# FFN output of a two-layer encoder trunk: x's sums added by on-chip transfers, and m2, v and h of two groups in shared banks

## Chip, cores and metric

The kernel runs on one core of one Trainium2 chip, as one program. The metric is the device time of one execution in microseconds (us), median of three runs. A profiled execution gives the trace: start and duration of every instruction on TensorE (PE; PEld is its weight load), VectorE (DVE), ScalarE (ACT), GpSimd (POOL), and the transfers issued from SyncE's queue (SP) and from POOL's.

## The reference

Two layers, each a token mixer with three branches and then a feed-forward network (FFN), on x of 512 rows by 1024 columns in float32. The part that the change touches is the second half of each layer:

```python
x = _layer_norm(DEEPNORM_ALPHA * x + mix, ln1_g[l], ln1_b[l])
u = jnp.einsum('bsd,df->bsf', x, w_ffn_in[l])
u_gate, u_up = jnp.split(u, 2, axis=-1)
ffn = jnp.einsum('bsf,fd->bsd', jax.nn.silu(u_gate) * u_up, w_ffn_out[l])
x = _layer_norm(DEEPNORM_ALPHA * x + ffn, ln2_g[l], ln2_b[l])
```

The hidden width is 2816, that is 22 tiles of 128. The last product, hidden (512 x 2816) by w_ffn_out (2816 x 1024), and the layer norm behind it are what is rearranged.

## The kernel before

**Numbers.** Each float32 operand is carried as a pair hi + lo, and each product of tiles is three matmuls, hi·hi, hi·lo and lo·hi (mm3, L120 to L122). A weight block is loaded into a staging buffer (tile st) and split: ScalarE casts it to hi (tile wh, L267, or L152 for blocks of w_ffn_in and w_in), then VectorE subtracts for lo (tile wl, L268 or L153). There are four staging buffers (NSTAGE) and three pairs wh and wl (AHEAD).

**Fewer products.** The hidden tiles are cut into three groups of consecutive tiles (GROUPS): 8, 8 and 6 tiles, called o, w and r here as in the code. In each group, the left operand and the weights are cut into 2 x 2 blocks, and seven products are formed in place of eight: m1, m2, y, x, v, g, h. Each is made twice (j = 0, 1, one for each tile of 128 rows of a half), into one PSUM bank of 128 x 512 (tile pf). With kh = 4 tiles of depth a product takes 2 x 12 matmuls, in r with kh = 3 it takes 2 x 9. The combinations of hidden tiles for the left side are made in s_hid (L300 to L303 and L112).

**Weights of a product.** Some products need sums of weight blocks. They are made by transfers that add onto a staging buffer: `load` (L172, SP's queue) brings a block, `more` (L176, POOL's queue, accumulating) adds another onto it. In a group's chain (class Chain, Fore for r) one staging buffer lives from m1 (Chain) or from `ahead_a` (Fore) to h: y, x and h each split it, and y and x then add the next block. `ahead_c` prepares the sum for g in a second buffer. m2 and v (and m1 of Fore) load a block each into whatever buffer is free, and release it when VectorE has split it.

**Sums.** z holds the rows of x: four tiles t of 128 rows, each in two halves hf of 512 columns. `plus` (L1316, or L1314 when a half of z is first touched and scaled by ALPHA) adds a bank or a tile onto a half of z on VectorE. m1 and y copy their banks to SBUF (tiles w and wy, L1341 and L1348, ScalarE). x computes u = x - m1 (L1354), adds it to z[2+j][0], then y + u (L1356), adds that to z[2+j][1] and z[j][1]. m2, v, g and h add their banks straight onto z. With the last product that touches a half, its statistics are taken (bn, L481). When both halves of a tile are there, it is normalised: `normalise` in layer 0 (L498 to L503, with one operation on POOL, L501), `finish` in layer 1 (L486 to L493, POOL L489), which also sends the rows out (L494).

**Order.** `items` is a list written out by hand: each entry names its weight blocks, the product, and groups of side work that are put between its two j or behind it. `run_items` fetches (loads and splits) blocks up to three ahead. A scheduler then places the instructions of each engine; SP's and POOL's queues run in their order as well. For w and r the order of products is: w.m1, u(19), w.y, u(20), w.x, u(21), w.m2, w.v, r.m1, r.y, w.g, r.m2, r.x, r.v, w.h, r.g, r.h. Here u(i) is a hidden tile of the first FFN product (u_ffn, 48 matmuls). In layer 0, s_norm(0) and s_norm(1), the transposes of the finished tiles 0 and 1 for the next layer (tile px, L512) and their split (to_T), stand between the two j of w.h and behind it; the next layer's first products need them.

```python
def take(self, i, j):
    b = self.block(self.a)
    self.more(self.a, i, j)
    return b
...
self.hi = wsp.tile([P, 2048], F32R, tag="wh", name="wh")[:, :n].rearrange("p (k c) -> p k c", k=nk)
...
nc.scalar.copy(self.hi, st)
nc.vector.tensor_sub(self.lo, st, f(self.hi))
```

Of the kernel before, what the change touches and what calls it, by code (L numbers as in the profile page):

```python
# [15 lines left out]
ALU = mybir.AluOpType  # L16

P = 128
# [36 lines left out]
def trunk(ctx, tc, x_in, xT_in, w_in, ret_norm_g, da_norm_g, lq1, lk1, lq2, lk2, w_a, w_b, w_c, b_merge, w_out,  # L55
          ln1_g, ln1_b, w_ffn_in, w_ffn_out, ln2_g, ln2_b, rel, rope_ret, rope_da, decay, out):
    nc = tc.nc
# [23 lines left out]
    def bank(name="ps"):  # L81
        return psp.tile([P, 512], F32, tag="ps", name=name)
# [36 lines left out]
    def mm3(ps, lh, ll, rh, rl, start, stop):  # L119
        nc.tensor.matmul(ps, lh, rh, start=start, stop=False)  # L120
        nc.tensor.matmul(ps, lh, rl, start=False, stop=False)  # L121
        nc.tensor.matmul(ps, ll, rh, start=False, stop=stop)  # L122
# [219 lines left out]
            self.part("g", self.a21)  # L342
            self.part("h", a22)

    def product(acts, name, j, wt):

        ps, sl = bank("pf"), slice(P * j, P * j + P)
        for k in range(wt.nk):
            hi, lo = acts[k].use[name]
            mm3(ps, hi[:, sl], lo[:, sl], wt.hi[:, k], wt.lo[:, k], k == 0, k == wt.nk - 1)  # L350
# [205 lines left out]
    def between():  # L556

        if pending:
            for fn in pending.pop(0):
                fn()  # L560
# [54 lines left out]
    def layer(l):  # L615
# [7 lines left out]
        v = {}  # L623
# [252 lines left out]
        def v_away(dst, wd):  # L876


            def done(t, c):
                for hf in range(2):  # L880
                    s = g(F32R, "vhl")
                    s3 = s.rearrange("p (h x) -> p h x", x=2 * wd)
                    src = c[:, 256 * hf:256 * hf + 256].rearrange("p (h x) -> p h x", x=wd)
                    part_hi(s3[:, :, 0:wd], src)
                    part_lo(s3[:, :, wd:2 * wd], src, s3[:, :, 0:wd])
                    dst[t, hf] = dram.tile([P, 512], F32, name=f"v{l}_{wd}_{t}_{hf}")
                    nc.sync.dma_start(dst[t, hf], f(s))
            return done
# [262 lines left out]
        x1 = {}  # L1151
# [50 lines left out]
        hid = [None] * FT  # L1202
# [5 lines left out]
        last = l == DEPTH - 1  # L1208
        x2 = {}
# [92 lines left out]
        def u_ffn(i):  # L1302
            def fn(wt):
                pg = proj_T(x1T, wt, 0)
                pu = proj_T(x1T, wt, P)
                ffn_done(i, pg, pu)
            return [ffn_spec(i)], fn

        def plus(t, hf, ps, op, final=False):

            z = x1["z"][t][hf]
            if (t, hf) in x2["fresh"]:
                x2["fresh"].remove((t, hf))
                nc.vector.scalar_tensor_tensor(z, z, ALPHA, ps, op0=ALU.mult, op1=op)  # L1314
            else:
                nc.vector.tensor_tensor(z, z, ps, op=op)  # L1316
            if final:
                x2["n"].stats(t, hf)

        def fout_items(gi):  # L1320


            r0, kh = GROUPS[gi]
            end = gi == len(GROUPS) - 1
            hv = (Fore if end else Chain)(w_ffn_out[l], r0, kh)
            w = {}

            def run(name, j, wt):
                return product([hid[r0 + k] for k in range(kh)], name, j, wt)

            def m1(wt):
                if gi == 0:
                    load_res(saved[2 * l])
                    x2["fresh"] = {(t, hf) for t in range(NT) for hf in range(2)}
                if end:
                    x2["n"] = Norm(x1["z"], v["g2"], v["b2"], bcast_rows(ln2_g[l:l + 1]),
                                   bcast_rows(ln2_b[l:l + 1]), xTs[l + 1], out if last else saved[2 * l + 1], xfs[l + 1])
                for j in range(2):
                    ps = run("m1", j, wt)
                    w[j] = g(name="w")  # L1340
                    nc.scalar.copy(w[j], ps)  # L1341
                    plus(j, 0, ps, ALU.add)

            def y(wt):
                for j in range(2):
                    ps = run("y", j, wt)
                    w["y", j] = g(name="wy")
                    nc.scalar.copy(w["y", j], ps)  # L1348

            def x(wt):  # L1350
                for j in range(2):
                    ps = run("x", j, wt)
                    u = w.pop(j)
                    nc.vector.tensor_sub(u, ps, u)  # L1354
                    plus(2 + j, 0, u, ALU.subtract)
                    nc.vector.tensor_add(u, u, w.pop(("y", j)))  # L1356
                    plus(2 + j, 1, u, ALU.add)
                    plus(j, 1, u, ALU.add)

            def normed(t):  # L1360
                (x2["n"].finish if last else x2["n"].normalise)(t)

            def one(name, i, hf):
                def fn(wt):
                    for j in range(2):
                        plus(2 * i + j, hf, run(name, j, wt), ALU.add, end)
                        if end and name != "m2":
                            normed(2 * i + j)
                        between()
                return fn  # L1370

            def gg(wt):
                for j in range(2):
# [4 lines left out]
            return {"c": hv.ahead_c, "a": getattr(hv, "ahead_a", None),  # L1378
                    "m1": ([hv.m1], m1), "y": ([hv.y], y), "x": ([hv.x], x), "m2": ([hv.m2], one("m2", 0, 0)),
                    "v": ([hv.v], one("v", 0, 1)), "g": ([hv.g], gg), "h": ([hv.h], one("h", 1, 0))}  # L1380

        def s_norm(t):
            def fn():
                if not last:
                    x2["n"].transposes(t)
                    if t:
                        x2["n"].to_T(0)
            return fn

        p, q, o, w, r = u_fin(0), u_fin(1), fout_items(0), fout_items(1), fout_items(2)  # L1390
        for (specs, fn), *groups in [
            (u_ffn_first([8, 9]), [s_natural(0)], [s_x1(0)]), (u_ffn(10), [s_x1(1), s_x1(2)], [s_x1(3), s_natural(1)]),
            (p["m1"], [s_natural(2)], [p["c"], s_natural(3)]), (u_ffn(11),), (p["y"],), (p["m2"],),
            (p["v"],), (p["x"],), (u_ffn(12), [], [s_turn(0, 0)]), (p["g"],), (p["h"],),
            (q["m1"], [], [q["c"]]), (u_ffn(13), [s_turn(0, 1)]), (q["y"],), (q["m2"],),
            (q["v"],), (q["x"],), (u_ffn(14), [], [s_turn(1, 0)]), (q["g"],), (q["h"], [s_ready(0)], [s_ready(1)]),
            (o["m1"], [], [s_turn(1, 1)]), (u_ffn(15), [s_twins(0)], [s_twins(1), o["c"]]), (o["m2"],), (o["y"],), (u_ffn(16),),
            (o["v"],), (o["x"],), (u_ffn(17),), (o["g"], [], [s_hid(1, 0)]), (o["h"], [], [s_hid(1, 1)]),
            (u_ffn(18), [s_hid(1, 2)], [s_hid(1, 3)]),
            (w["m1"],), (u_ffn(19),), (w["y"],), (u_ffn(20),), (w["x"], [s_hid(2, 0), r["a"]]),  # L1400
            (u_ffn(21), [s_hid(2, 1), w["c"]]), (w["m2"], [s_hid(2, 2)]), (w["v"],),
            (r["m1"],), (r["y"],), (w["g"], [], [r["c"]]), (r["m2"],), (r["x"],), (r["v"],),
            (w["h"], [s_norm(0)], [s_norm(1)]), (r["g"],), (r["h"],),
        ]:
            item(specs, fn, *groups)

# [8 lines left out]
    for l in range(DEPTH):  # L1415
        layer(l)
# [48 lines left out]
```

## Time and profile before

| What | Value |
|---|---|
| time, median of 3 runs | 1901.95 us (1901.42 to 1902.55) |
| profiled execution, its own time | 1901.65 us |
| its span | 1899.9 us |
| mean granted clock of TensorE | 0.995 |
| instructions | 24193 |
| moved by transfers | 292.98 MB, 154 GB/s on average |

The span is the trace's own clock; 1.75 us of the execution lie around it. A row of a timeline gives the start, the duration, the engine, the line of the code, what is written and read, and in brackets the idle time of the engine ahead of it with what ended it. Matmuls overlap, so the pace of TensorE is the distance of their starts, not their duration. The row "DMA to landing" gives the time from a transfer's issue until its data are there. "PEclk" is the clock that TensorE was granted, 1.00 being full.

### The profile page before, as it was taken

To read this page: it belongs to the slowest core of one execution; us is meant where nothing else is said; L and a number is where in the kernel's file an instruction comes from. 1 tells how busy PE (TensorE), PEld (TensorE's weight loads), DVE (VectorE), ACT (ScalarE), POOL (GpSimd) and SP (SyncE) were. 2 spreads that over 40 slices of the span, in tenths; PEclk is the share of its full clock that TensorE was granted. 3 is DMA by queue.
4 is the path that set the end of the run, shared out by engine and by line. 5 is a ranking of instruction groups with operands and counts; after the bars stand their busy time and mean duration, and the time that the engine had idled before them with its cause. 6 is when DMAs were issued, how large, how long until landed. Compare 5 with 4: busy or idle time off the path is not lost. (4 is left out here: it accounts for less than half of the span.)

```text
span 1899.9 us, 24193 instructions
## 1 busy us (share of the span) xinstructions
PE 1874.6 (99%) x9134; PEld 1579.8 (83%) x9134; DVE 1391.4 (73%) x2221; ACT 962.5 (51%) x1593; POOL 124.4 (7%) x149
## 2 busy tenths in 40 slices
PE   9999999999999999999899999999999999999996
PEld 7888888888888888888798888888888898888885
DVE  6788866677666856787887788566775668677878
ACT  5555554576634444444455556555765344344441
POOL 2000000000000000001020000000000000000001
PEclk9999999999999999999999999999999999999998
DMA  9584443332254687756765944532322637776574
GB/s 289 173 274 134 138 156 114 103 122 67 82 187 120 166 189 172 192 141 162 193 188 171 279 118 144 172 100 95 122 78 73 214 91 184 173 192 183 132 171 113
DMA packets 243350, 292.98 MB, mean 154 GB/s; under 512 B 8741, under 2 KB 148097, under 8 KB 243233
## 3 DMA queue, kind: packets, MB, share of 16 engines
q1 hardware_dynamic: 216032, 238.58, 38.4%
q0 software_dynamic: 27200, 52.85, 16.5%
q8 instruction: 72, 1.18, 0.3%
q14 instruction: 46, 0.37, 0.1%
HBM read 268.28 MB, written 23.12 MB: 153 GB/s over the span
## 5 line engine op out<-in xcount | busy, mean ns | idle before, releaser
L120 PE MATMUL pt<-xTh,wh 128*128 128x512 f32 (+1 forms) x1328 | 497.9, 375 | 0.5 <-ACT wh L152 0.3
L122 PE MATMUL pt<-xTh,wl 128*128 128x512 f32 (+1 forms) x1328 | 493.7, 372 | 0.0
L121 PE MATMUL pt<-xTl,wh 128*128 128x512 f32 (+1 forms) x1328 | 493.1, 371 | 0.0
L268 DVE TENSOR_TENSOR wl<-st,wh 128x2048 fp32r<-128x2048 f32 (+1 forms) x112 | 248.8, 2221 | 113.2 <-ACT wh L267 112.6
L267 ACT CAST wh<-st 128x2048 fp32r<-128x2048 f32 (+1 forms) x112 | 208.2, 1859 | 184.2 <-PE pf L122 69.2
L153 DVE TENSOR_TENSOR wl<-st,wh 128x1024 fp32r<-128x1024 f32 (+1 forms) x220 | 243.0, 1122 | 66.7 <-ACT wh L152 60.5
L152 ACT CAST wh<-st 128x1024 fp32r<-128x1024 f32 (+1 forms) x220 | 208.3, 971 | 155.9 <-PE pt L121 58.8
L122 PEld LDWEIGHTS pt<-xTh,wl 128*128 128x128 f32 x1328 | 250.1, 188 | 43.7
L120 PEld LDWEIGHTS pt<-xTh,wh 128*128 128x128 f32 x1328 | 250.3, 189 | 42.9 <-ACT wh L152 1.1
L121 PEld LDWEIGHTS pt<-xTl,wh 128*128 128x128 f32 x1328 | 250.4, 189 | 41.5
L122 PE MATMUL pf<-wh,xTl 128*128 128x512 f32 x240 | 93.4, 389 | 0.0
L121 PE MATMUL pf<-wl,xTh 128*128 128x512 f32 x240 | 93.4, 389 | 0.0
L120 PE MATMUL pf<-wh,xTh 128*128 128x512 f32 x240 | 93.4, 389 | 0.0
L120 PE MATMUL pf<-wh,s43h 128*128 128x512 f32 x216 | 84.9, 393 | 0.0
L120 PE MATMUL pf<-wh,s12h 128*128 128x512 f32 x216 | 84.2, 390 | 0.0
L121 PE MATMUL pf<-wl,s43h 128*128 128x512 f32 x216 | 84.1, 390 | 0.0
L122 PE MATMUL pf<-wh,s12l 128*128 128x512 f32 x216 | 84.1, 389 | 0.0
L121 PE MATMUL pf<-wl,s12h 128*128 128x512 f32 x216 | 84.1, 389 | 0.0
L122 PE MATMUL pf<-wh,s43l 128*128 128x512 f32 x216 | 83.3, 390 | 0.0
L390 ACT COPY sw<-pt 32x512 f32<-32x512 f32 (+1 forms) x96 | 55.6, 579 | 27.1 <-PE pt L122 25.9
L176 POOL DMA_DIRECT2D st<-in_w_ffn_out x24 | 30.8, 1297 | 349.8 <-DVE wl L268 226.7
L1215 DVE TENSOR_TENSOR fth<-fth,pt 128x512 f32<-128x512 f32 x28 | 19.2, 686 | 45.9 <-PE pt L122 45.6
(354 smaller groups left out, 3567.5 us busy)
## 6 DMA issues: line engine op xcount, KB each, us to landing
st<-in_w_in SPq DMA_DIRECT2D x60, 1024.0 KB, 5.2
st<-in_w_ffn_in SPq DMA_DIRECT2D x56, 512.0 KB, 5.4
st<-in_w_in SPq DMA_DIRECT2D x32, 512.0 KB, 5.2
st<-in_w_ffn_in SPq DMA_DIRECT2D x16, 1024.0 KB, 6.0
st<-in_w_ffn_in POOLq DMA_DIRECT2D x16, 1024.0 KB, 9.3
st<-in_w_ffn_out SPq DMA_DIRECT2D x16, 1024.0 KB, 5.3
st<-in_w_ffn_out POOLq DMA_DIRECT2D x16, 1024.0 KB, 8.7
st<-in_w_in POOLq DMA_DIRECT2D x12, 1024.0 KB, 11.4
```

The source lines that it names most:

```text
L120: nc.tensor.matmul(ps, lh, rh, start=start, stop=False)
L121: nc.tensor.matmul(ps, lh, rl, start=False, stop=False)
L122: nc.tensor.matmul(ps, ll, rh, start=False, stop=stop)
L152: return [nc.scalar.copy(self.hi[:, a:b], self.st[:, a:b]), nc.vector.tensor_sub(self.lo[:, a:b], self.st[:, a:b], f(self.hi[:, a:b]))]
L153: nc.vector.tensor_sub(self.lo[:, a:b], self.st[:, a:b], f(self.hi[:, a:b]))]
L176: nc.gpsimd.dma_start(t, self.src(i, j), accum_op=ALU.add)
L267: nc.scalar.copy(self.hi, st)
L268: nc.vector.tensor_sub(self.lo, st, f(self.hi))
L390: nc.scalar.copy(sw[half * b:half * b + half], ps[half * o:half * o + half])
L1215: nc.vector.tensor_mul(t, t, pu)
```

## The change

In x, both combinations change sign and place (u = m1 - x, y = y - u). In the first group (o) all sums go onto z as before. In w and r the three sums of each j are no longer added by VectorE: three accumulating transfers from POOL's queue add u and y, 256 KB each, onto the halves of z. m2 and v of w leave their banks open; the same product of r goes on in them, and VectorE adds the common bank once. h of w and h of r are one item of two blocks (both_h), j by j in one bank. The order of products becomes: w.m1, u(19), w.y, u(20), w.x, u(21), w.g, r.m1, r.y, w.m2, r.m2, r.x, w.v, r.v, r.g, h of both. `ahead_c` of w moves two items up, that of r too, `ahead_a` of r one. s_norm(0) stands behind r.g, s_norm(1) between the two j of h.

```diff
-    def product(acts, name, j, wt):
-        ps, sl = bank("pf"), slice(P * j, P * j + P)
+    def product(acts, name, j, wt, ps=None, stop=True):
+        start, sl = ps is None, slice(P * j, P * j + P)
+        ps = bank("pf") if start else ps
...
             def x(wt):
                 for j in range(2):
                     ps = run("x", j, wt)
-                    u = w.pop(j)
-                    nc.vector.tensor_sub(u, ps, u)
-                    plus(2 + j, 0, u, ALU.subtract)
-                    nc.vector.tensor_add(u, u, w.pop(("y", j)))
-                    plus(2 + j, 1, u, ALU.add)
-                    plus(j, 1, u, ALU.add)
+                    u, y = w.pop(j), w.pop(("y", j))
+                    nc.vector.tensor_sub(u, u, ps)
+                    nc.vector.tensor_sub(y, y, u)
+                    for t, hf, d in ((2 + j, 0, u), (j, 1, y), (2 + j, 1, y)):
+                        if gi == 0:
+                            plus(t, hf, d, ALU.add)
+                        else:
+                            nc.gpsimd.dma_start(x1["z"][t][hf], d, accum_op=ALU.add)
...
-                        plus(2 * i + j, hf, run(name, j, wt), ALU.add, end)
-                        if end and name != "m2":
-                            normed(2 * i + j)
+                        if gi == 0:
+                            plus(2 * i + j, hf, run(name, j, wt), ALU.add)
+                        elif not end:
+                            x2[name, j] = run(name, j, wt, None, False)
+                        else:
+                            plus(2 * i + j, hf, run(name, j, wt, x2.pop((name, j))), ALU.add, True)
+                            if name == "v":
+                                normed(j)
                         between()
...
+        def both_h(w, r):
+            def fn(*wts):
+                for j in range(2):
+                    ps = w["run"]("h", j, wts[0], None, False)
+                    plus(2 + j, 0, r["run"]("h", j, wts[1], ps), ALU.add, True)
+                    normed(2 + j)
+                    between()
+            return [w["hv"].h, r["hv"].h], fn
...
-            (w["m1"],), (u_ffn(19),), (w["y"],), (u_ffn(20),), (w["x"], [s_hid(2, 0), r["a"]]),
-            (u_ffn(21), [s_hid(2, 1), w["c"]]), (w["m2"], [s_hid(2, 2)]), (w["v"],),
-            (r["m1"],), (r["y"],), (w["g"], [], [r["c"]]), (r["m2"],), (r["x"],), (r["v"],),
-            (w["h"], [s_norm(0)], [s_norm(1)]), (r["g"],), (r["h"],),
+            (w["m1"],), (u_ffn(19), [w["c"]]), (w["y"],), (u_ffn(20), [r["a"]]), (w["x"], [s_hid(2, 0)]),
+            (u_ffn(21), [s_hid(2, 1)]), (w["g"], [], [s_hid(2, 2)]),
+            (r["m1"], [r["c"]]), (r["y"],), (w["m2"],), (r["m2"],), (r["x"],), (w["v"],), (r["v"],),
+            (r["g"], [s_norm(0)]), (both_h(w, r), [s_norm(1)]),
```

More of the change, by code (lines that the diff above doesn't have):

```diff
@@ L343, in sums @@
             self.part("h", a22)
-    def product(acts, name, j, wt):
-        ps, sl = bank("pf"), slice(P * j, P * j + P)
+    def product(acts, name, j, wt, ps=None, stop=True):
+        start, sl = ps is None, slice(P * j, P * j + P)
+        ps = bank("pf") if start else ps
         for k in range(wt.nk):
             hi, lo = acts[k].use[name]
-            mm3(ps, hi[:, sl], lo[:, sl], wt.hi[:, k], wt.lo[:, k], k == 0, k == wt.nk - 1)
+            mm3(ps, hi[:, sl], lo[:, sl], wt.hi[:, k], wt.lo[:, k], start and k == 0, stop and k == wt.nk - 1)
         return ps
@@ L1326, in fout_items, with run @@
             w = {}
-            def run(name, j, wt):
-                return product([hid[r0 + k] for k in range(kh)], name, j, wt)
+            def run(name, j, wt, *ps):
+                return product([hid[r0 + k] for k in range(kh)], name, j, wt, *ps)
             def m1(wt):
@@ L1352, in x @@
                     ps = run("x", j, wt)
-                    u = w.pop(j)
-                    nc.vector.tensor_sub(u, ps, u)
-                    plus(2 + j, 0, u, ALU.subtract)
-                    nc.vector.tensor_add(u, u, w.pop(("y", j)))
-                    plus(2 + j, 1, u, ALU.add)
-                    plus(j, 1, u, ALU.add)
-            def normed(t):
-                (x2["n"].finish if last else x2["n"].normalise)(t)
+                    u, y = w.pop(j), w.pop(("y", j))
[6 more added lines that the diff above has]
+                            nc.gpsimd.dma_start(x1["z"][t][hf], d, accum_op=ALU.add)
             def one(name, i, hf):
@@ L1376, in gg, with normed @@
                     plus(2 + j, 0, ps, ALU.subtract)
-            return {"c": hv.ahead_c, "a": getattr(hv, "ahead_a", None),
+            return {"c": hv.ahead_c, "a": getattr(hv, "ahead_a", None), "run": run, "hv": hv,
                     "m1": ([hv.m1], m1), "y": ([hv.y], y), "x": ([hv.x], x), "m2": ([hv.m2], one("m2", 0, 0)),
                     "v": ([hv.v], one("v", 0, 1)), "g": ([hv.g], gg), "h": ([hv.h], one("h", 1, 0))}
+        def normed(t):
+            (x2["n"].finish if last else x2["n"].normalise)(t)
+        def both_h(w, r):
[6 more added lines that the diff above has]
+            return [w["hv"].h, r["hv"].h], fn
         def s_norm(t):
```

## The prediction

> **What bounds the kernel now.** I read the page first, then the busy time by stretches, then the timelines of the ends of the two layers, engine by engine. The page shows TensorE busy for 99% of the span:
>
> ```profile
> PE 1874.6 (99%) x9134; PEld 1579.8 (83%) x9134; DVE 1391.4 (73%) x2221; ACT 962.5 (51%) x1593; POOL 124.4 (7%) x149
> ```
>
> Only 25 us of the 1899.9 are left for a change that removes no product, and this one removes none. The stretches tell where they are (length, then busy us of PE, PEld, DVE, ACT, POOL, granted clock, DMA share, GB/s):
>
> ```profile
> 930.00:945.00 15.00, 11.69 (x49) 9.91 (x50) 9.57 (x18) 4.50 (x8) 1.10 (x2) 0.77 0.41 128
> 1880.00:1899.90 19.90, 4.09 (x19) 3.04 (x17) 16.79 (x32) 0.00 (x0) 2.81 (x3) 0.69 0.28 106
> ```
>
> One hole is at the end of layer 0, the other is the tail. TensorE's timeline at the first (start, duration, what):
>
> ```profile
> 926.38 0.39 PE L122 MATMUL pf<-wh,q2l 128*128 128x512 f32 x1
> 933.31 1.97 PE L512 MATMUL px<-ident,z 128*128 128x128 f32 x8 [6.55 <-DVE z L503]
> 934.93 0.78 PE L120 MATMUL pf<-wh,q2h 128*128 128x512 f32 x1
> ...
> 938.73 0.40 PE L120 MATMUL pf<-wh,q2h 128*128 128x512 f32 x1
> 938.96 0.39 PE L121 MATMUL pf<-wl,q2h 128*128 128x512 f32 x1
> 939.42 1.03 PE L512 MATMUL px<-ident,z 128*128 128x128 f32 x8
> 940.21 0.48 PE L120 MATMUL pf<-wh,s43h 128*128 128x512 f32 x1
> ```
>
> TensorE waits 6.55 us for the normalised rows of tile 0. Then it runs slow: the transposes take 0.94 us more than at 939.42, and the nine matmuls from 934.93 to 938.73 take 3.80 us where nine at full pace take 2.04. The loss is 6.55 + 0.94 + 1.76 = 9.25 us. Layer 1 has no such hole, but its tail:
>
> ```profile
> 1833.61 0.39 PE L120 MATMUL pf<-wh,q2h 128*128 128x512 f32 x1
> ...
> 1879.85 0.39 PE L120 MATMUL pf<-wh,q2h 128*128 128x512 f32 x1
> ...
> 1883.70 0.39 PE L122 MATMUL pf<-wh,q2l 128*128 128x512 f32 x1
> ```
>
> The last product (18 matmuls from 1879.85) gives the pace, (1883.70 - 1879.85)/17 = 0.2265 us, so a product of w (24 matmuls) takes 5.44, one of r (18) 4.08. TensorE is through at 1883.9; VectorE is behind:
>
> ```profile
> 1866.59 1.28 DVE L1354 TENSOR_TENSOR w<-pf,w 128x512 f32<-128x512 f32 x2
> ...
> 1870.19 2.49 DVE L1316 TENSOR_TENSOR z<-z,w 128x512 f32<-128x512 f32 x4
> 1872.60 1.75 DVE L268 TENSOR_TENSOR wl<-st,wh 128x1536 fp32r<-128x1536 f32 x1
> ...
> 1888.67 1.27 DVE L1316 TENSOR_TENSOR z<-z,pf 128x512 f32<-128x512 f32 x2
> 1889.85 1.28 DVE L481 BATCH_NORM_STATS2 bn<-z 128x6 f32<-128x512 f32 x2
> ...
> 1895.38 1.41 DVE L493 SCALAR_TENSOR_TENSOR z<-z,rs,bc 128x512 f32<-128x512 f32 x2
> ```
>
> From 1866.59 to 1872.60 it works off x of r, ten operations at 0.60 us apart; the last additions start at 1888.67, 4.7 us after TensorE's end, and from 1889.85 to the end of the span (1899.9) pass 10.05 us.
>
> **The change, part by part.** *VectorE.* Per layer, x of w and of r lose three additions for each of two j (12), and m2, v, h of w lose their own (6): 18 of 0.60 us, 10.8 us, 21.6 in both layers. All but those in the two holes lie under TensorE and are worth nothing. x of the first group keeps its ten operations. The shared banks hold m2's and v's two banks one product longer; no product finds them short, as each is followed by its partner or by r's x.
>
> *Transfers.* 12 of 256 KB per layer go to POOL's queue. No row of before shows one on chip. The nearest:
>
> ```profile
> st<-in_w_ffn_out POOLq DMA_DIRECT2D x16, 1024.0 KB, 8.7
> ...
> saved<-z SPq DMA_DIRECT2D x24, 256.0 KB, 3.5
> ...
> st<-in_w_ffn_out POOLq DMA_DIRECT2D x8, 768.0 KB, 7.6
> ```
>
> 256 KB less is 1.1 us less, so 7.6 - 2.2 = 5.4 us for one alone; the ends are 3.5 and 8.7. Six behind each other add 1.1 each. The additions of g of w wait for those of x of w, 10.9 us (the 48 matmuls of u_ffn(21)) after x ends: hidden. Those of v of r wait for the fifth of r's, about 5.4 + 4.4 = 9.8 us after the first issue, while v of w and r give TensorE 9.5 us: just covered. The hidden pieces for (2,1) and (2,2) now also wait for the freed x tiles, with more than 3 us of slack.
>
> *The order.* Here I see the cost. Only four staging buffers (st) exist. From m1 of r on, w's chain (held for h), r's chain and the held sum for g of r take three; so m2 of w, m2 of r, v of w and v of r all go through the fourth, each load starting when VectorE has split the one before. Before, the same buffer served v of w, m1, m2 and v of r, further apart. What one hop takes is shown by (SP's or POOL's issue, then its time to landing; ACT's cast; DVE's split):
>
> ```profile
> 1821.57 0.37 SPq L172 DMA_DIRECT2D st<-in_w_ffn_out  x1
> DMA to landing us min/median/max: 5.0/5.0/5.0
> ...
> 1827.17 1.28 POOL L176 DMA_DIRECT2D st<-in_w_ffn_out  x1 [20.38 <-DVE sb L303]
> 1831.06 0.37 SPq L172 DMA_DIRECT2D st<-in_w_ffn_out  x1
> DMA to landing us min/median/max: 6.6/6.6/6.6
> ...
> 1840.99 0.37 SPq L172 DMA_DIRECT2D st<-in_w_ffn_out  x1
> DMA to landing us min/median/max: 4.5/4.5/4.5
> ...
> 1858.79 1.48 ACT L267 CAST wh<-st 128x1536 fp32r<-128x1536 f32 x1 [2.55 <-DMA st<-in_w_ffn_out]
> 1860.34 1.75 DVE L268 TENSOR_TENSOR wl<-st,wh 128x1536 fp32r<-128x1536 f32 x1
> ...
> 1817.31 1.91 ACT L267 CAST wh<-st 128x2048 fp32r<-128x2048 f32 x1 [3.83 <-issue]
> 1819.25 2.29 DVE L268 TENSOR_TENSOR wl<-st,wh 128x2048 fp32r<-128x2048 f32 x1 [1.08 <-ACT wh L267]
> ```
>
> 1 MB lands in 5.0 us. 768 KB land in 4.5, and in 6.6 beside an adding transfer of 1 MB (1827.17). From landing to the split's end pass 1862.09 - 1858.7 = 3.4 us for 768 KB and 1.91 + 0.1 + 2.29 = 4.3 for 1 MB.
>
> The chain in before's clock of layer 1: g of w now starts at 1833.61 (m2's place) and ends at 1839.05, then m1 and y of r end at 1843.13 and 1847.21. A cast must wait for the product three places ahead (three buffers), so m2 of w is cast from 1839.1; with g's additions ahead of its split it is through at 1843.6. Then m2 of r: load 5.0 (between 4.5 and 6.6, with y's adding transfer in flight at first), 3.4: 1852.0. Due when m2 of w ends, 1852.65: on time. Then v of w: 5.1, 4.3: 1861.4. Due when x of r ends, 1860.81: 0.6 late. Then v of r: 6.8, as x's own adding transfer (768 KB) and then the six new ones run beside it, 3.4: 1871.6. Due when v of w ends, 1861.4 + 5.44 = 1866.85: 4.75 late.
>
> So TensorE starts v of r at 1871.6 and not at 1866.25. The same holds in layer 0, whose rows repeat these 946.45 us earlier:
>
> ```profile
> 924.08 1.49 ACT L267 CAST wh<-st 128x1536 fp32r<-128x1536 f32 x1 [2.60 <-PE pf L122]
> ...
> 1870.53 1.49 ACT L267 CAST wh<-st 128x1536 fp32r<-128x1536 f32 x1 [2.60 <-PE pf L122]
> ```
>
> *Layer 1.* After v of r come g (4.08) and the pair h (42 matmuls, 9.52): TensorE ends at 1871.6 + 17.7 = 1889.3, 5.4 later than before. VectorE needs about as long: after r.h's split (1879.3) finish(0), finish(1), four additions and two statistics fill 10 us. Then one addition and the 10.05 of the row at 1889.85: 1889.3 + 0.2 + 0.6 + 10.05 = 1900.15, and 0.15 for the backlog: +0.4 on 1899.9. The tail shrinks by as much as the stall grows.
>
> *Layer 0.* v of r starts at 925.15. VectorE then splits g and h of w (3.9), adds v's two products (to 5.3), takes statistics, splits h of r (7.6), and with one more statistics, addition and the 0.92 of two normalising rows has tile 0 ready 9.9 after 925.15; g of r ends after 8.16, so the transposes wait 1.75. Twice 0.8 of transposes and 9.52 of h: end at 925.15 + 8.16 + 1.75 + 1.6 + 9.52 = 946.2. Before: 940.21 + 2 x 4.08 = 948.4. That is -2.2; the second weight block of the next layer now finds its buffer 2 us ahead of its first use, not 4, for which I give back 0.4: -1.8.
>
> *The clock after the stall.* The stall of 6.55 us cost 0.94 + 1.76 = 2.7. A stall of 4.75 has no row; its ends are 0 and 2.7. It lies nearer to 6.55 than to none, but nothing shows where the drop begins, so I take half, 1.3, in each layer: +2.6. The Trainium skill (TensorE: Matmul & The Clock Gate, "Part 1: The HAM clock gate") says that the clock halves after at least one idle window of about 3.4 us, and that these windows run freely. The trace agrees at 6.55 us. By that rule, as an estimate, 4.75 us hold a whole window in (4.75 - 3.41)/3.41 = 39% of the phases, and the sum would be 0.5 us lower.
>
> In sum, +0.4 - 1.8 + 2.6 = +1.2 on the profiled execution's 1901.65 (span 1899.9 and 1.75 around it): 1902.8. The runs' median is 0.3 above that execution. I call within 0.2% what lies within 3.8 us of the median 1901.95; about that much can be told from no change.
>
> **The rivals.** *A: the loads land early and the relief of VectorE decides.* With 4.5, 5.0, 4.5 (14.0 in place of 16.9) v of r starts at 1868.7, the stall is about 2, the clock holds: 2 x 2.9 + 2.6 = 8.4 less, 1894.4. With no stall at all it is 2 x 2.4 less again, 1889.6. For it: each of these times has a row. Against it: 4.5 was seen with no adding transfer at its start, and v of r has them throughout. 0.27.
>
> *B, on the slower side: the new transfers hold up the load of v of r.* Beside 1 MB of adding transfer a load took 2.1 us more; beside 768 KB and 1.5 MB it would take 2.1 x 2.25 = 4.7 more, 9.2 in place of 6.8. Each layer is 2.4 later and the stall 7.1, long enough for the whole clock loss: 2 x 2.4 + 2.8 = 7.6 more, 1910.4. It decides from a landing of about 8 us on. Against it: POOL issues the six over some 4 us, so part of them comes after the load. 0.26.
>
> *C: VectorE waits for the transfers, so that they do not relieve it.* At 8.7 and not 5.4 the fifth lands 3.3 later, and behind the waiting addition of v stand the statistics and the split of h of r, which has 3.1 us of slack. About 2 us per layer: 1907. 0.07.
>
> **How the numbers follow.** The forecast's case has 0.40: none, one or both of the stalls losing the clock give 1900.2, 1902.8 and 1905.5, all within 0.2%. A is faster (0.27), B and C slower (0.33). The range reaches into A and B, 1895 to 1911, and leaves out a tenth on either side.
>
> **What would show it.** On TensorE, a wait of 4 to 5 us ahead of v of r in both layers, released by the cast or split of its weights, and 1.7 us ahead of the first transposes; one staging buffer's loads each issued as the split before ends; landings near 5.0, 5.1 and 6.8; the last addition within 1 us of TensorE's end. A gap-free TensorE there, or additions of v waiting for a transfer, would prove it wrong.

## The result, and the profile after

The changed kernel takes 1904.52 us (median of 20 runs, 1901.28 to 1908.71), the kernel before 1901.53 (20 runs, 1900.39 to 1903.77): a ratio of 1.0015, with a 95% interval of 1.0008 to 1.0022. That is 3.0 us, within the 0.2% that the prediction called no difference, though the interval lies wholly above 1: a small slowdown. The forecast was 1902.8. The profiled execution took 1902.72 us (before 1901.65), its span is 1900.9.

The page after, busy time of the engines:

```profile
PE 1876.0 (99%) x9134; PEld 1577.9 (83%) x9134; DVE 1371.0 (72%) x2185; ACT 965.1 (51%) x1593; POOL 145.6 (8%) x173
```

VectorE has 20.4 us less to do (1391.4 before; the working said 21.6), and the time has not followed. The stretches, with the columns as in the prediction (length, PE, PEld, DVE, ACT, POOL, granted clock, DMA share, GB/s):

```profile
930.00:945.00 15.00, 13.30 (x68) 10.89 (x67) 14.09 (x28) 6.38 (x10) 1.65 (x3) 1.00 0.94 305
1880.00:1900.90 20.90, 9.60 (x43) 7.62 (x41) 17.54 (x34) 0.00 (x0) 3.82 (x4) 0.83 0.27 101
```

The old hole at the end of layer 0 is filled (13.30 us of 15 in place of 11.69, at the full clock), and TensorE now works into what was the tail. Its timeline shows what it waits for instead; first the rows of layer 0, then those of layer 1:

```profile
907.38 0.50 PE L121 MATMUL pf<-wl,q2h 128*128 128x512 f32 x1 [0.96 <-DVE wl L268]
...
916.78 0.50 PE L121 MATMUL pf<-wl,s43h 128*128 128x512 f32 x1 [0.90 <-DVE wl L268]
...
924.08 0.73 PE L120 MATMUL pf<-wh,s43h 128*128 128x512 f32 x2 [1.78 <-ACT wh L267]
925.46 0.73 PE L120 MATMUL pf<-wh,s43h 128*128 128x512 f32 x2 [0.65 <-ACT wh L267]
...
935.18 1.11 PE L513 MATMUL px<-ident,z 128*128 128x128 f32 x8 [1.70 <-DVE z L504]
...
1852.52 0.50 PE L121 MATMUL pf<-wl,q2h 128*128 128x512 f32 x1 [1.29 <-DVE wl L268]
...
1862.00 0.50 PE L121 MATMUL pf<-wl,s43h 128*128 128x512 f32 x1 [1.02 <-DVE wl L268]
...
1869.68 1.12 PE L120 MATMUL pf<-wh,s43h 128*128 128x512 f32 x2 [2.15 <-ACT wh L267]
1871.05 1.22 PE L120 MATMUL pf<-wh,s43h 128*128 128x512 f32 x2 [0.26 <-ACT wh L267]
...
1889.21 0.39 PE L122 MATMUL pf<-wh,q2l 128*128 128x512 f32 x1
```

Three waits in each layer, ahead of m2 of r, v of w and v of r: 4.3 us in layer 0, 4.7 in layer 1. In layer 1 the matmuls from 1869.68 also run slow (1.12 us for two where layer 0 shows 0.73). All are waits for weights, for ScalarE's cast (tile wh) or VectorE's subtraction (tile wl). VectorE's tail:

```profile
1889.42 1.27 DVE L1317 TENSOR_TENSOR z<-z,pf 128x512 f32<-128x512 f32 x2
1890.61 1.28 DVE L482 BATCH_NORM_STATS2 bn<-z 128x6 f32<-128x512 f32 x2
```

The last additions now start 0.2 us after TensorE's last matmul starts (nearly 5 us after it before). TensorE ends 5.5 us later than before, the last additions start 0.75 us later. What was gained at the old hole and in the tail was spent ahead of m2 and v.

### The profile page after: what moved, and what is told of

Read it like the earlier page. It is cut to its first block, busy times and chain, and to the rows that moved or that the text cites. A ratio compares the mean times of both kernels' runs of the same rounds, so it can differ in the third digit from the quotient of the medians.

```text
span 1900.9 us, 24201 instructions
## 1 busy us (share of the span) xinstructions
PE 1876.0 (99%) x9134; PEld 1577.9 (83%) x9134; DVE 1371.0 (72%) x2185; ACT 965.1 (51%) x1593; POOL 145.6 (8%) x173
## 5 line engine op out<-in xcount | busy, mean ns | idle before, releaser
L120 PEld LDWEIGHTS pf<-wh,s43h 128*128 128x128 f32 x216 | 40.7, 190 | 15.0 <-ACT wh L267 6.8
```

## The experiments

Theory 1 is the forecast's: blocks loaded one after the other into one staging buffer make TensorE wait. Theory 2: the transfers on chip are what costs, by slowing loads or by keeping VectorE waiting. Theory 3: relief of VectorE is worth nothing. Each kernel ran beside the kernel before; every ratio is to that, with its 95% interval. Differences between two experiments are differences of their medians.

### x of w and r by VectorE, all else as after

```diff
-                        if gi == 0:
-                            plus(t, hf, d, ALU.add)
-                        else:
-                            nc.gpsimd.dma_start(x1["z"][t][hf], d, accum_op=ALU.add)
+                        plus(t, hf, d, ALU.add)
```

> The kernel after in its order and with its shared banks, but the sums of x of w and r are added by VectorE (12 additions of 0.60 us per layer more, no transfers on chip). Theory 1: the waits ahead of m2 of r and v of w stay; v of w's split comes behind some of r's six additions (up to 3.6 us) while the load of v of r is up to 1.6 us shorter, so the wait ahead of v of r grows by about 2 us and costs the clock in both layers: 1907 to 1913 us. Theory 2: without the transfers the load of v of r takes 4.5 us and not 6.1, the wait shrinks, and the time falls to 1899 to 1902. Theory 3 (VectorE's additions lie hidden in either form): within 2 us of the kernel after.

1899.43 us, ratio 0.9989 (0.998 to 0.9997): faster than before, and 5.1 us below the kernel after. Theory 2 was right; the time lies at the low end of its range. The issues between 1817 and 1832 us tell where the load of the block for g of r suffers. The kernel after (GB/s in 40 slices of the 15 us, then KB each and us to landing):

```profile
GB/s 0 0 0 44 0 0 0 0 0 11 98 11 317 388 426 410 404 388 366 246 202 197 208 202 202 208 202 202 224 175 186 208 175 240 208 279 240 279 279 257
...
z<-wy POOLq DMA_DIRECT2D x4, 256.0 KB, 8.0
st<-in_w_ffn_out SPq DMA_DIRECT2D x1, 768.0 KB, 9.9
```

With VectorE's additions:

```profile
GB/s 22 0 0 0 0 0 44 0 0 0 27 27 76 333 415 393 410 421 399 295 0 0 0 0 0 0 0 0 0 0 0 0 0 0 38 0 126 399 360 404
...
st<-in_w_ffn_out SPq DMA_DIRECT2D x1, 768.0 KB, 4.4
```

A load alone moves about 400 GB/s; beside adding transfers the sum of both falls to about 200. The block for g of r lands after 9.9 us and not 4.4. Its adding step is then issued together with that of r's y (POOL's row at 1835.48 holds both; they land after 7.6 and 11.3 us), and both run beside the load of m2 of r. SP's timeline in layer 1, first of the kernel after, then of the one with VectorE's additions:

```profile
1841.68 0.37 SPq L172 DMA_DIRECT2D st<-in_w_ffn_out  x1
DMA to landing us min/median/max: 7.4/7.4/7.4
```

```profile
1843.16 0.37 SPq L172 DMA_DIRECT2D st<-in_w_ffn_out  x1
DMA to landing us min/median/max: 4.5/4.5/4.5
```

m2 of r lands after 7.4 us and not 4.5. In the same view the load of v of r, beside r's own transfers, takes 6.1 and not 4.7.

The additions given back to VectorE cost nothing; its timeline in that kernel shows why:

```profile
1864.16 0.68 DVE L1317 TENSOR_TENSOR z<-z,w 128x512 f32<-128x512 f32 x1
1864.76 1.28 DVE L1317 TENSOR_TENSOR z<-z,wy 128x512 f32<-128x512 f32 x2
1866.81 5.63 DVE L268 TENSOR_TENSOR wl<-st,wh 128x1536 fp32r<-128x1536 f32 x3 [0.77 <-ACT wh L267]
```

These are the last three of r's six additions. All six fit between the split of v of w and the next row, that of v of r, and VectorE still stands idle for 0.77 us. In the kernel after it stands idle there for 5.31 us. What theory 1 expected of this run, additions that delay the split of v of w, did not happen.

### The transfers alone, in the order and with the banks of before

```diff
-                    nc.vector.tensor_sub(u, ps, u)
-                    plus(2 + j, 0, u, ALU.subtract)
...
+                            nc.gpsimd.dma_start(x1["z"][t][hf], d, accum_op=ALU.add)
```

> The kernel before in its order and with a bank of its own for each product, but the three sums of x of w and r are added by transfers on chip: the one part of the change alone. Theory 1: VectorE is 3.6 us less behind after x of r in each layer, so the wait of 6.55 us ahead of the first transposes in layer 0 shrinks to about 3 and loses less clock, and the last additions come 3.6 us earlier in layer 1: 1891 to 1896 us, faster than both kernels. Theory 2: the additions of v and g wait for the transfers, or loads become late: 1901 to 1906. Theory 3: relief of VectorE is worth nothing, within 2 us of the kernel before (1901.5).

1914.32 us, ratio 1.0064 (1.0052 to 1.0077): 12.4 us slower than before, the opposite of what theory 1 gave, and beyond the others. VectorE at the end of layer 0, in that kernel:

```profile
937.90 0.69 DVE L1316 TENSOR_TENSOR z<-z,pf 128x512 f32<-128x512 f32 x1 [7.12 <-DMA z<-wy]
```

TensorE behind it:

```profile
944.10 1.97 PE L512 MATMUL px<-ident,z 128*128 128x128 f32 x8 [13.07 <-DVE z L503]
```

The additions of v wait 7.12 us for the transfers onto the same rows, and the hole ahead of the transposes doubles, from 6.55 to 13.07 us. That is the prediction's rival C, in the old order. In the new one v of r comes later, and nothing waits.

### One half of the transfers each

In the first, only w keeps them, in the second only r.

```diff
-                        if gi == 0:
+                        if gi != 1:
```

```diff
-                        if gi == 0:
+                        if not end:
```

> The kernel after, but only x of w adds its sums by transfers; those of x of r are added by VectorE. Theory 2, made sharper by the runs so far (a transfer on chip occupies the DMA engines and slows the loads beside it): the six transfers of w slow the load of the block for g of r (9.9 us in the kernel after, 4.4 with VectorE's additions), so its adding step comes together with that of r's y and the load of m2 of r; the wait of 1.0 to 1.3 us ahead of m2 of r stays in each layer, that ahead of v of r is the 1.6 to 1.9 us of the kernel with VectorE's additions. 1901 to 1903 us. Theory 1 (the one staging buffer causes the waits by itself): the wait ahead of m2 of r has nothing to do with w's transfers, so the time is that of the kernel with VectorE's additions plus the share of VectorE's relief, 1898 to 1900.

> The other half: only x of r adds its sums by transfers, those of x of w are added by VectorE. Theory 2: no wait ahead of m2 of r, load of v of r 5.8 to 6.2 us and a wait of about 2.4 ahead of it: 1901 to 1903 us, so that the two halves together make up the 5.1 us between the kernel after and the one with VectorE's additions. Theory 1: waits as in the kernel after ahead of m2 of r too, 1903 to 1905.

1903.44 (ratio 1.0007, 0.9997 to 1.0016) and 1903.22 us (1.0006, 0.9997 to 1.0015). Each costs about 4 us over the 1899.43 without transfers, both together 5.1: they do not add up. The waits stand where theory 2 put them. TensorE's waits by releaser (us in total, times, longest) with w's transfers:

```profile
PE pf L121 <- DVE wl L268: 4.4, 4, 1.3
PE pf L120 <- ACT wh L267: 4.1, 4, 1.7
```

and with r's:

```profile
PE pf L120 <- ACT wh L267: 6.1, 4, 3.0
...
PE pf L121 <- DVE wl L268: 1.3, 2, 0.7
```

With w's, all four waits for a split (m2 of r and v of w) are there; with r's, those ahead of m2 of r are gone, and those ahead of v of r come to 6.1 us in the two layers, 3.0 at the longest, where about 2.4 per layer was expected. Both medians are 0.2 to 0.4 us above the expected range.

### The order alone

VectorE adds x's sums, and every product has a bank of its own. (In the list, `ahead_c` of w moves up by four entries, from u(21) to u(19), and not by two.)

```diff
+                        plus(2 * i + j, hf, run(name, j, wt), ALU.add, end)
+                        if end and name == "v":
+                            normed(j)
...
+                    plus(2 + j, 0, w["run"]("h", j, wts[0]), ALU.add)
+                    plus(2 + j, 0, r["run"]("h", j, wts[1]), ALU.add, True)
```

> The new order alone: the sums of x are added by VectorE, and m2, v and h of w have banks of their own, each added onto the rows by itself (6 additions of 0.60 us per layer more than with shared banks). If the shared banks carry the gain over the kernel before: VectorE comes later to the splits of m2 and v of r, by up to 1.2 us each, 1901 to 1904 us. If the order carries it (VectorE stands idle ahead of those splits for 0.8 to 4.8 us): 1898 to 1901 us.

1904.55 us, ratio 1.0009 (1.0 to 1.0017; 1899.19 to 1905.97): 5.1 us above the same kernel with shared banks, 1.6 between the fastest runs. The median is 0.55 us above the range for shared banks that carry the gain. They do carry it, but not through the splits of m2 and v as expected: the waits for weights hardly move. It is the first transposes of layer 0 that wait longer (TensorE's timeline):

```profile
934.61 1.11 PE L513 MATMUL px<-ident,z 128*128 128x128 f32 x8 [2.88 <-DVE z L504]
```

They wait 1.68 us with shared banks; the last of the experiments shows VectorE's part in that. The tail of layer 1 grows too: from TensorE's last matmul to the end of the span pass 13.2 us, 11.4 with shared banks. The 5.1 us between the medians are more than these 2.9. Much of the rest goes with the clock, of which each run has its mean on record: at 0.998 the two kernels lie 1.1 us apart (medians of 2 and 4 runs), and the nine other runs of the kernel with banks of its own have 0.994 to 0.997. What lost the clock in them no trace shows.

### A second staging buffer for m2 and v

The sum for g of r is begun later, so that m2 of w, m2 of r, v of w and v of r alternate between two buffers. First with the transfers of the kernel after, then with VectorE's additions.

```diff
-            (r["m1"], [r["c"]]), (r["y"],), (w["m2"],), (r["m2"],), (r["x"],), (w["v"],), (r["v"],),
+            (r["m1"],), (r["y"],), (w["m2"],), (r["m2"],), (r["x"], [r["c"]]), (w["v"],), (r["v"],),
```

> The kernel after, but the sum of blocks for g of r is begun with x of r and not with m1 of r, so that a second staging buffer is free for m2 of w, m2 of r and v of w, which then alternate between two. Theory 1: the waits ahead of m2 of r and v of w go (2 us per layer), that ahead of v of r shrinks or goes (2.4), and what may come is a wait ahead of g of r, whose sum takes two further adding steps of about 6 us each: up to 3 us. In all 1896 to 1903 us. Theory 2: nothing changes ahead of v of r, and r's late adding steps collide with the transfers of x: 1904 to 1908. Theory 3: within 2 us of the kernel after.

> The kernel after with the sums of x by VectorE and the sum of blocks for g of r begun with x of r, g of r still ahead of the common h: the version of 1893.3 us without its exchange of g and h. Theory 1 with 2: no wait ahead of m2, v of w and v of r; the adding step for g lands about 7.4 us after its issue, so that about 1.5 us of wait come ahead of g of r in each layer: 1896 to 1900 us. If the exchange of g and h was worth nothing: 1893 to 1894.

1903.31 (ratio 1.0004, 0.9995 to 1.0013) and 1905.29 us (1.0016, 1.0008 to 1.0025). The first is 0.3 us above theory 1's range, and within the 2 us of the kernel after that theory 3 gave. In both the three waits are gone, as theory 1 said, and a wait ahead of g of r takes their place. TensorE in the second:

```profile
928.35 0.75 PE L120 MATMUL pf<-wh,s43h 128*128 128x512 f32 x1 [2.36 <-ACT wh L267]
930.14 0.79 PE L121 MATMUL pf<-wl,s43h 128*128 128x512 f32 x1 [1.04 <-DVE wl L268]
```

That makes 3.4 us in layer 0, and 3.9 in layer 1 (2.59 and 1.30), where 1.5 was expected for the second kernel; that expectation was wrong, and the kernel is slower than with one buffer. The last two adding steps take 7.6 to 9.1 us each in layer 1 of the two kernels, not about 6.

Between these two the transfers show no price. With them TensorE waits longer ahead of g of r (8.4 us in the two layers, 7.2 without), and yet that kernel is the faster by 2.0 us; its runs have granted clocks of 0.994 to 0.997, those of the other 0.993 to 0.996. Theory 2 alone does not explain this pair, and the cause stays open.

### The buffer taken out of the way otherwise

m2 and v of r are loaded as three pieces of 256 KB into free row buffers, and do not need a staging buffer.

```diff
+            ts = [g(name="sx") for _ in range(nk)]
+            for k, t in enumerate(ts):
+                nc.sync.dma_start(t, src[:, k])
...
+                nc.scalar.copy(self.hi[:, k], t)
+                nc.vector.tensor_sub(self.lo[:, k], t, f(self.hi[:, k]))
```

> The kernel after, but m2 and v of r are loaded as three separate pieces of 256 KB into free row buffers, so that they no longer go through the fourth staging buffer (casts and splits become three small ones each). Theory 1 (the forecast: loads that follow each other in one staging buffer cause the waits): TensorE's waits ahead of m2 of r, v of w and v of r (0.96 + 0.90 + 2.4 us in layer 0; 1.29 + 1.02 + 2.4 us and some clock in layer 1) are gone, so 4 us per layer and the clock losses of some runs: 1893 to 1897 us. Theory 2 (the transfers on chip slow the loads, whatever buffer they go to, or make VectorE wait): a wait of 2 us or more stays ahead of v of r, time within 2 us of the kernel after (1902 to 1906). Theory 3 (relieving VectorE is worth nothing, its work is late anyway): the waits ahead of the products go but come back ahead of the transposes and in the tail, time within 2 us of the kernel before.

1910.49 us, ratio 1.0041 (1.0029 to 1.0054): against theory 1, and above what the others expected. The timeline of TensorE:

```profile
912.02 1.08 PE L120 MATMUL pf<-wh,q2h 128*128 128x512 f32 x2 [3.70 <-ACT wh L244]
941.70 1.97 PE L533 MATMUL px<-ident,z 128*128 128x128 f32 x8 [6.01 <-DVE z L524]
```

The six pieces stand on SP's queue behind the load of v of w, and land 7.2 us after their issue (median in layer 0); m2 of r is 3.7 us late in one piece, 4.4 in layer 1. Then nothing ahead of v of r covers the transfers, and an addition of v waits 4.33 us for them. It tests the buffer badly, because it changes the order of the loads too; it does show the second limit behind the first.

### h ahead of g: a version faster than both

VectorE's additions, shared banks, the second buffer, and the common h ahead of g of r, which gives the sum for g 9.5 us more.

```diff
-            (r["g"], [s_norm(0)]), (both_h(w, r), [s_norm(1)]),
+            (both_h(w, r), [s_norm(0)], [s_norm(1)]), (r["g"],),
...
-                    plus(2 + j, 0, ps, ALU.subtract)
+                    plus(2 + j, 0, ps, ALU.subtract, end)
+                    if end:
+                        normed(2 + j)
```

> A version that may beat both: sums of x by VectorE, shared banks, the sum of blocks for g of r begun with x of r (so that m2 of w, m2 of r, v of w and v of r alternate between two staging buffers), and the product g of r behind the common h, so that its sum has 9.5 us more. Theory 1 with theory 2 (waits come from loads behind each other in one buffer, made longer by transfers): no wait ahead of m2, v or g; about 1 us ahead of the first transposes in layer 0; one statistics and one addition more behind the last product, 1.2 us: 1893 to 1897 us. If VectorE is late by then (finish of tiles 0 and 1 beside h) the tail gives it back: 1898 to 1900.

1893.30 us, ratio 0.9951 (0.9938 to 0.9964): 8.5 us under the kernel before in the same runs. Of the waits of TensorE (us in total, times, longest) this is the only one above half a microsecond in the part that was rearranged:

```profile
PE px L513 <- DVE z L504: 1.8, 3, 1.3
```

Three more kernels take one thing away from it each. First VectorE's additions, for the transfers of the kernel after:

> The version of 1893.3 us, but with the transfers on chip of the kernel after in place of VectorE's additions. Nothing waits there for a staging buffer, so this tells whether the transfers cost anything without the chain of loads. Theory 1 (the chain is what turns late loads into waits): the loads still take 6 to 10 us beside the transfers, but no product waits for them: within 1.5 us of 1893.3. Theory 2 in its strong form (transfers cost by themselves): 4 to 6 us more, 1897 to 1899, with waits of VectorE for the transfers or of TensorE ahead of v or g.

1907.18 us, ratio 1.0029 (1.0018 to 1.004): 13.9 us more. Theory 1 alone is refuted by this, and theory 2 underrated. VectorE waits for the transfers (layer 0):

```profile
930.23 0.69 DVE L1317 TENSOR_TENSOR z<-z,pf 128x512 f32<-128x512 f32 x1 [4.87 <-DMA z<-wy]
...
935.44 0.69 DVE L1317 TENSOR_TENSOR z<-z,pf 128x512 f32<-128x512 f32 x1 [3.79 <-DMA z<-wy]
```

and TensorE for VectorE:

```profile
939.63 1.97 PE L513 MATMUL px<-ident,z 128*128 128x128 f32 x8 [8.74 <-DVE z L504]
```

The transfers share the DMA engines with four blocks of 1 MB for the next layer, and land late (issues from 914 to 940 us, then KB each and us to landing):

```profile
st<-in_w_in SPq DMA_DIRECT2D x4, 1024.0 KB, 10.3
z<-wy POOLq DMA_DIRECT2D x4, 256.0 KB, 12.0
```

These blocks are not the whole cause. In layer 1 none follow, and the four transfers from wy still land after 10.1 us (median); VectorE waits 4.28 and 2.43 us for them. In both layers the adding step for g of r, 768 KB, stands directly ahead of them on POOL's queue (919.17 and 1869.06). The kernel after, which begins that sum early, has no such step there. So the 13.9 us price the transfers together with the late sum, not by themselves.

Second, the later start of the sum for g (it is begun with m1 of r again, so that one buffer serves all four blocks):

> The version of 1893.3 us, but with the sum of blocks for g of r begun with m1 of r as in the kernel after, so that one staging buffer serves m2 of w, m2 of r, v of w and v of r again; sums of x by VectorE, h ahead of g. Theory 1: the waits of the kernel with VectorE's additions are back, 0.7 us ahead of v of w and 1.6 to 1.9 ahead of v of r in each layer, some of them at the cost of the clock: 1897 to 1901 us. If the gain came from the exchange of g and h and not from the second buffer: 1893 to 1895.

1902.55 us, ratio 1.0 (0.9991 to 1.0009): 9.3 us more. The waits are back:

```profile
PE pf L121 <- DVE wl L268: 3.3, 4, 1.1
PE pf L120 <- ACT wh L267: 2.8, 2, 1.9
```

6.1 us in the two layers together; in each layer the granted clock also falls to 0.50 for 3.4 us, behind these waits. The median is 1.6 us above the expected range, the sign as theory 1 said. ScalarE's cast for v of r in layer 1 shows that the turn of the buffer makes the wait, and not how long the load takes, first with one buffer, then in the faster kernel with two:

```profile
1866.96 3.27 ACT L267 CAST wh<-st 128x1536 fp32r<-128x1536 f32 x2 [8.28 <-DMA st<-in_w_ffn_out]
```

```profile
1850.51 1.49 ACT L267 CAST wh<-st 128x1536 fp32r<-128x1536 f32 x1 [2.12 <-PE pf L122]
```

With one buffer the load takes 5.6 us, and ScalarE stands idle for it. With two it takes 8.7, but is issued at 1840.74 in place of 1861.24, and has landed 1.1 us ahead of the cast, which waits for TensorE to free a buffer wh. Third, the shared banks:

> The version of 1893.3 us, but m2, v and h of w and of r have banks of their own again (6 additions of 0.60 us per layer more), nothing else changed; no product waits for a staging buffer there, so this prices the shared banks alone. If they carry what they did between the kernels with one buffer (5.1 us between medians, 1.6 between the fastest runs): 1895 to 1898 us, the wait ahead of the first transposes in layer 0 growing from 1.3 us to 2.5 to 3, the additions of v of w standing between x of r and the splits for v and h. If VectorE's time is hidden: within 1 us of 1893.3.

1894.87 us, ratio 0.9967 (0.9954 to 0.9979): 1.6 us more between the medians, 4.0 between the fastest runs (1894.78 and 1890.80). With one buffer it was the other way round, 5.1 and 1.6, so the price of the banks is known no better than that. VectorE's additions after the splits for v of r and h, in the faster kernel:

```profile
924.71 1.27 DVE L1317 TENSOR_TENSOR z<-z,pf 128x512 f32<-128x512 f32 x2
```

and with banks of their own:

```profile
924.97 2.48 DVE L1317 TENSOR_TENSOR z<-z,pf 128x512 f32<-128x512 f32 x4
```

Two additions more, those of v of w, stand ahead of tile 0's statistics, and TensorE waits 1.2 us longer for the transposes:

```profile
931.72 1.11 PE L513 MATMUL px<-ident,z 128*128 128x128 f32 x8 [2.47 <-DVE z L504]
```

2.47 us where the faster kernel waits 1.27. The tail of layer 1 grows as well, from 12.2 us behind TensorE's last matmul to 14.2. So theory 3 is wrong at these two places, where VectorE is last. The median is 0.1 us under the expected range.

## Why the prediction came out

**What held.** *The chain.* The forecast had v of r start 5.35 us late in each layer, through loads that follow each other in the fourth staging buffer. The waits came to 4.3 and 4.7 us, all for a cast or a split. That the buffer's turn causes them is shown: with two buffers they are gone in five kernels, and with one they return in a kernel that is otherwise the fastest. (That a wait ahead of g takes their place in two of the five does not touch this.) *The tail* shrank by nearly as much as the stalls grew, the last additions starting 0.2 us after TensorE's last matmul starts. *Layer 0* gained 1.7 us by the same row of both layers (before, the prediction's two casts lie 946.45 us apart), 1.8 forecast:

```profile
892.63 1.92 ACT L267 CAST wh<-st 128x2048 fp32r<-128x2048 f32 x1 [2.08 <-PE pf L122]
...
1837.37 1.92 ACT L267 CAST wh<-st 128x2048 fp32r<-128x2048 f32 x1 [2.10 <-PE pf L122]
```

These are 944.74 apart. *The transposes* waited 1.70 us, 1.75 forecast. *The clock* was lost in one of the two stalls of the profiled execution, the middle one of the forecast's three cases; the loss is 1.0 us (from 1869.68 the eighth matmul starts after 3.62 us, the same one in layer 0 after 2.65), where the forecast took 2.7 for a full loss.

**Where the wait lies.** The forecast put 4.75 us ahead of v of r, 0.6 ahead of v of w and none ahead of m2 of r. Measured are 2.4, about 1.0 and about 1.1. The step that failed is the load of m2 of r, "5.0 (between 4.5 and 6.6, with y's adding transfer in flight at first)": it took 7.0 and 7.4 us, since two adding steps and not one ran beside it. The second is the sum for g of r, which the step did not count at all: w's transfers had delayed its load to 9.9 us. On the other side the load of v of r took 5.7 and 6.1, not 6.8, and TensorE started on v of r when the cast was done, 1.6 us after the landing, where the working counted 3.4, to the split's end. So in layer 1 2.4 us too little stands against 0.7 and 1.8 too much, and v of r starts at 1869.68, or 1871.4 with layer 0's 1.7 us added back, against 1871.6 forecast. That this came so close is luck.

**The sum.** The profiled execution's 1902.72 us against 1902.8 is luck in part too. With its share of the clock, 1.3 per layer, the forecast had -0.5 for layer 0 and +1.7 for layer 1. Measured are -1.7, as no clock was lost there, and +2.7, the rest of the 1.0 by which the span grew. The median of the 20 runs is 1.7 us above the forecast.

**The transfers' price.** "5.4 us for one alone" and 1.1 more for each behind it was too low: medians of 6.4 to 9.0 us in the kernel after, 7.3 to 10.8 at the end of layer 0 in the old order, 12.0 where the adding step for g of r stands ahead of them and loads for the next layer run beside them. "Just covered" was right for a reason that the working had not given: v of r is late, so its additions are late too. With two buffers v of r is on time and the transfers land later as well, and the cover is gone (waits of 4.87 and 3.79 us).

**The rivals.** A: the loads do not land in the times that it needs, and relief of VectorE decides nothing behind them. With VectorE's additions they do land so (4.5, 5.1 and 4.7 us in layer 1), and about 2.3 us of waits stay in that layer, close to A's 2; the time is 1899.43, not A's 1894.4. B has the right resource, and the wrong victim: the load of v of r loses 1.4 us to the transfers and not the 4.7 that B added, but the block for g of r loses 5.5, and m2 of r 2.9 (layer 1). C does not decide in this order; it decides in the old one.

**Taken apart.** The kernel before took 1901.5 to 1901.9 us (medians); the order alone makes it 1904.55, shared banks on top 1899.43, the transfers on top of both 1904.52. The last two parts cancel. By the fastest runs the same steps are 1900.4, 1899.2, 1897.6 and 1901.3, so the order's own part even changes its sign. The median of the kernel after stands 1.8 us above its profiled execution; that goes with the clock. The nine fastest of its 20 runs (up to 1903.3 us) have a mean granted clock of 0.997 or 0.998, the eleven others (from 1904.3) 0.995 or 0.996. The five runs of the version without stalls all have 0.998, and spread over 2.8 us, not 7.4. In which stalls a run without a trace lost it is not known.

## What to carry to other kernels

A transfer that adds on chip takes work from an engine, and puts it on the DMA engines that bring the weights: before moving an addition there, look at what lands next to it and who is waiting for that. Here the same 24 transfers cost from nothing to 13.9 us, by what stood beside them. When one limit hides another, removing either shows nothing or a loss (from the kernel with VectorE's additions: the second buffer alone 5.9 us more, h ahead of g alone 3.1 more, both together 6.1 less): follow the next wait in the trace, and try the two together. Relief of an engine counts only where that engine, and not what it waits for, is last; idle time of 5 us ahead of its next split is the sign that it isn't.

## What was not expected of the hardware

**The rate of adding transfers.** The slices of the kernel after show about 200 GB/s while on-chip additions and a load run together, with the DMA engines over 90% busy, and about 400 for a load alone. The Trainium skill (DMA: Bandwidth & Descriptors, "Issuing engines are not separate DMA queues") says that transfers from all issuing engines run on the same 16 DMA engines and interleave. The runs agree: POOL's additions stretched SP's load from 4.4 to 9.9 us.

**The clock.** It was lost after waits far shorter than the 6.55 us before. TensorE in layer 1 of the kernel in which w alone keeps its transfers:

```profile
1867.23 0.39 PE L122 MATMUL pf<-wh,s43l 128*128 128x512 f32 x1
1868.76 0.73 PE L120 MATMUL pf<-wh,s43h 128*128 128x512 f32 x2 [1.13 <-ACT wh L267]
1870.13 1.22 PE L120 MATMUL pf<-wh,s43h 128*128 128x512 f32 x2 [0.64 <-ACT wh L267]
1871.15 0.63 PE L121 MATMUL pf<-wl,s43h 128*128 128x512 f32 x1
1871.58 0.63 PE L122 MATMUL pf<-wh,s43l 128*128 128x512 f32 x1
```

The two stretches of 3.4 us around the drop (columns as in the prediction):

```profile
1866.70:1870.10 3.40, 1.66 (x7) 0.72 (x5) 2.73 (x4) 2.87 (x3) 0.00 (x0) 1.00 0.00 1
1870.10:1873.50 3.40, 3.37 (x8) 2.69 (x9) 3.40 (x3) 1.78 (x1) 0.00 (x0) 0.50 0.00 0
```

Until 1870.1 the granted clock is 1.00, then 0.50 for 3.4 us, and TensorE takes 0.43 us from one matmul to the next in place of 0.2265. In the 3.4 us ahead of the drop it was busy for 1.66, and no single wait was over 1.13 us. Waits of 0.99 and 0.64 us, in layer 1 with VectorE's additions, kept the clock, and so did the longer ones of 1.78 and 0.65 us in layer 0 of the kernel after. The Trainium skill (TensorE: Matmul & The Clock Gate, "Part 1: The HAM clock gate") speaks of an idle window of about 3.4 us that runs freely. The 3.4 us at half clock agree with that length, but the stretch ahead of them was only half idle. How much idle time it takes was not measured; the prediction's estimate from the length of a single wait does not hold.
